# A kurtosis kernel whose first load is cut into pieces of 1024 and 3072 columns

## The chip, the cores and the metric

The kernel runs on one core of one Trainium2 chip. The metric is device time in microseconds (us): the median of several runs of one launch. The span of a profile runs from the first to the last instruction; it is about 1.7 us shorter than the measured time of the same run. All runs told here were fast: none was more than 1.5% above the fastest of its kernel. What is read inside a kernel's run comes from its one profile, so it carries that run's chance.

## The reference

```python
def reference(x):                        # x: 1024 x 8192, float32
    mean = np.mean(x, axis=-1, keepdims=True)
    std = np.std(x, axis=-1, keepdims=True)
    z = (x - mean) / (std + 1e-8)
    return (np.mean(z ** 4, axis=-1) - 3).astype(np.float32)
```

33.6 MB are read once, 4 KB are written.

## The kernel before

The rows go through in 16 groups of 64. Each row is laid over two partitions, so a group fills 128 partitions with 4096 columns (2.10 MB, 16 KB per partition). Five buffers hold the groups in flight. A group's table entry gives its rows' split over partitions, the pieces of its load, ScalarE's share of the fourth powers, and the engine that makes its mean.

```python
GROUPS = [
    (2, [4096], 1280, 'DVE'),
    (2, [4096], 1280, 'DVE'),
    (2, [4096], 768, 'DVE'),
    (2, [4096], 1536, 'DVE'),
    (2, [2304, 1792], 640, 'PE'),
    # ... seven more in two pieces, three of [1536, 1536, 1024], one in four pieces
]

def load(i):
    k, pieces = GROUPS[i][:2]
    w = n_cols // k
    xt = slots[SLOT_OF[i]]
    src = x[ROWS[i]:ROWS[i + 1], :].rearrange("r (k w) -> (r k) w", k=k)
    c = 0
    for w in pieces:
        nc.sync.dma_start(out=xt[:, c:c + w], in_=src[:, c:c + w])
        c += w

def added_halves(i, c):                  # VectorE: the mean's sum, for 'DVE' groups
    t = xts[i][:, c:]
    h = t.shape[1] // 2
    ...  # one instruction: sum of t[:, :h] + t[:, h:]

for i in range(L):                       # L = 15, the last group is treated apart
    mean(i)                              # VectorE or TensorE sums, TensorE over partitions, ScalarE copies
    square(i)                            # ScalarE, (x - mean)^2 in place
    if i >= 1:
        fourth_dve(i - 1, GROUPS[i - 1][2])   # VectorE
        load_next(i - 1)                 # the buffer of group i-1 is free: load into it
    ...
    fourth_act(i, 0, GROUPS[i][2])       # ScalarE
```

## Time and profile before

| | before |
|---|---|
| time, median of the first 3 runs | 97.04 us (97.0 to 97.14) |
| span of the profile | 95.2 us |
| ScalarE (ACT) busy | 79.8 us (84%) |
| VectorE (DVE) busy | 72.7 us (76%) |
| TensorE matmuls (PE) busy | 59.5 us (62%) |
| transfers, 16 DMA engines | 85.6% of the span, 33.56 MB |

No engine is full over the whole span, because the first 12 us are a start-up: until the first group is there nothing can be computed. After that ScalarE and the transfers are both nearly full. The waits of ScalarE say the same (engine, line, waited for: us in total, times, longest):

```profile
ACT nmu L176 <- PE mps L165: 9.4, 1, 9.4
ACT nmu L176 <- PE mps L174: 1.1, 1, 1.1
```

The reader is to see one wait for the first mean, one of 1.1 us in the middle, and no other that counts. nmu is the negative mean of a group, the last thing that ScalarE needs before it squares the group. In the lines below, junk is the unused output of VectorE's mean, tps holds TensorE's transposes, red VectorE's sums of them, and mps TensorE's sums over partitions; SPq is the issue of a load.

### The profile page before, as it was taken

Reading aid. Unit: us, or ns where it says so; the run is one execution under the profiler, and the core shown is the slowest. Engines: PE = TensorE matmul, PEld = TensorE weight load, DVE = VectorE, ACT = ScalarE, POOL = GpSimd, SP = SyncE. Lnnn points to the kernel's source line nnn. Section 1 sums busy time; section 2 is a strip of 40 time slices with the busy share of each in tenths; the row PEclk is TensorE's granted clock in tenths of the full one; section 3 lists DMA queues with packets and bytes.
Section 4 is the critical chain, followed back from the end, with each engine's and each line's share of the span. In section 5 each row is a group of like instructions: output and inputs, shape, how many; then the busy total and the mean of one; then the engine's idle time right before and its main releaser. Section 6 shows DMA issues by size and latency. Waiting matters only on the chain.

```text
span 95.2 us, 1248 instructions
## 1 busy us (share of the span) xinstructions
PE 59.5 (62%) x450; PEld 52.5 (55%) x450; DVE 72.7 (76%) x63; ACT 79.8 (84%) x88; POOL 2.7 (3%) x12
## 2 busy tenths in 40 slices
PE   0000202001089797979796969797979797989770
PEld 0000202001089696969695959686969696874330
DVE  2003529999995294979797979897999698999970
ACT  6000099999999779999999999999999999999970
POOL 6400000000000000000000000000000000000000
PEclk9999999999999999999999999999999999999999
DMA  4799999999999999999999999999999999700000
GB/s 89 268 433 433 433 427 433 440 433 394 425 429 413 425 428 429 412 422 412 433 409 430 424 419 420 415 408 403 423 412 420 416 407 408 276 15 0 0 0 1
DMA packets 4789, 33.63 MB, mean 353 GB/s; under 512 B 560, under 2 KB 560, under 8 KB 3248
## 3 DMA queue, kind: packets, MB, share of 16 engines
q1 hardware_dynamic: 4784, 33.56, 85.6%
q8 instruction: 3, 0.05, 0.2%
q14 instruction: 2, 0.02, 0.1%
HBM read 33.55 MB, written 0.00 MB: 352 GB/s over the span
## 4 chain that ended last, share of the span: by engine, by line
PE 26%; DMA 24%; ACT 18%; DVE 18%; issue 11%; SPq 0%; DVEq 0%
DMA xt<-in_x_dram 24%; PE tps L138 21%; ACT xt L182 16%; DVE xt L194 7%; DVE junk L155 7%; DVE red L144 2%; PE mps L174 2%; ACT xt L189 1%; PE pk L240 1%; PE mps L165 1%; PE pf L232 1%; SPq L132 0%; ACT nmu L176 0%; DVE q L194 0%; PE p L222 0%
## 5 line engine op out<-in xcount | busy, mean ns | idle before, releaser
L182 ACT ACTIVATE xt<-xt,nmu 128x4096 f32<-128x4096 f32 (+1 forms) x17 | 59.8, 3516 | 0.5
L194 DVE CUSTOM_DVE_ANT_0 xt<-xt 128x3456 f32<-128x3456 f32 (+8 forms) x17 | 57.5, 3386 | 2.3 <-ACT xt L182 1.9
L138 PE MATMUL tps<-ident,xt 128*128 128x128 f32 x380 | 46.9, 282 | 0.5 <-DMA xt<-in_x_dram 0.5
L138 PEld LDWEIGHTS tps<-ident,xt 128*128 128x128 f32 x380 | 43.9, 147 | 1.8 <-DMA xt<-in_x_dram 0.9
L165 PE MATMUL mps<-part,blk 128*128 128x1 f32 x8 | 2.3, 351 | 24.8 <-DVE part L155 24.8
L155 DVE CUSTOM_DVE_ANT_0 junk<-xt 128x2048 bf16<-128x2048 f32 (+1 forms) x5 | 9.6, 1915 | 9.9 <-DMA xt<-in_x_dram 9.9
L165 PEld LDWEIGHTS mps<-part,blk 128*128 128x128 f32 x8 | 2.0, 311 | 25.0 <-issue 11.0
L189 ACT ACTIVATE xt<-xt 128x640 f32<-128x640 f32 (+7 forms) x16 | 13.9, 870 | 0.5
L176 ACT COPY nmu<-mps 128x1 f32<-128x1 f32 x16 | 2.4, 148 | 10.7 <-PE mps L165 9.4
L144 DVE TENSOR_REDUCE red<-tps 128x128 f32<-128x256 f32 x12 | 5.1, 424 | 6.7 <-PE tps L138 6.6
L174 PEld LDWEIGHTS mps<-negcol,red 128*128 128x128 f32 x22 | 3.3, 188 | 8.9 <-issue 3.3
L174 PE MATMUL mps<-negcol,red 128*128 128x1 f32 x22 | 3.9, 249 | 6.5 <-DVE red L144 5.3
L203 PE MATMUL idle<-zeros 128*128 128x512 f32 x10 | 4.8, 609 | 0.0
L182 ACT ACTIVATION_READ_ACCUMULATOR xt<-xt,nmu 128x1 f32 x17 | 3.1, 184 | 0.0
L189 ACT ACTIVATION_READ_ACCUMULATOR xt<-xt 128x1 f32 x16 | 3.0, 186 | 0.0
L203 PEld LDWEIGHTS idle<-zeros 128*128 128x128 f32 x10 | 1.7, 191 | 1.4 <-issue 1.4
L67 ACT ACT_TABLE_LOAD x1 | 1.3, 1283 | 0.8 <-PEq L301 0.8
L194 DVE DVE_READ_ACCUMULATOR2_ANT q<- 128x1 f32 x17 | 1.4, 83 | 0.0
L218 PEld LDWEIGHTS p<-s,blk 128*128 128x128 f32 x4 | 0.7, 189 | 1.2 <-ACT xt L182 0.7
L66 DVE MEMSET zeros<- 128x512 f32 x1 | 0.5, 485 | 1.0 <-PEq L301 1.0
L218 PE MATMUL p<-s,blk 128*128 128x1 f32 x4 | 0.7, 234 | 0.7 <-ACT xt L182 0.7
L240 PE MATMUL pk<-blk,q 128*5 128x64 f32 (+1 forms) x10 | 1.0, 219 | 0.0
(32 smaller groups left out, 10.5 us busy)
## 6 DMA issues: line engine op xcount, KB each, us to landing
xt<-in_x_dram SPq DMA_DIRECT2D x8, 1152.0 KB, 11.4
xt<-in_x_dram SPq DMA_DIRECT2D x4, 2048.0 KB, 14.5
xt<-in_x_dram SPq DMA_DIRECT2D x8, 896.0 KB, 13.3
xt<-in_x_dram SPq DMA_DIRECT2D x7, 768.0 KB, 11.1
xt<-in_x_dram SPq DMA_DIRECT2D x3, 512.0 KB, 12.5
xt<-in_x_dram SPq DMA_DIRECT2D x1, 640.0 KB, 12.0
xt<-in_x_dram SPq DMA_DIRECT2D x1, 384.0 KB, 12.4
xt<-in_x_dram SPq DMA_DIRECT2D x1, 256.0 KB, 11.3
```

The costliest lines, as they stand in the source:

```text
L138: nc.tensor.matmul(tps, lhsT=xts[i][:, c:c + P], rhs=ident, start=c == 0, stop=c == w - P, is_transpose=True)
L144: nc.vector.tensor_reduce(out=red.rearrange("p (r k) -> p r k", k=2), in_=tps.rearrange("p (r k) -> p r k", k=2).unsqueeze(2).to_broadcast ...
L155: nc.vector.tensor_tensor_reduce(out=junk[:, :h], in0=t[:, :h], in1=t[:, h:], scale=1.0, scalar=0.0, op0=AO.add, op1=AO.add, accum_out=part)
L165: nc.tensor.matmul(mps, lhsT=blk[k], rhs=added_halves(i, 0), start=True, stop=True)
L174: nc.tensor.matmul(mps, lhsT=pair_sums(tps), rhs=negcol, start=True, stop=True)
L176: nc.scalar.copy(nmu, mps)
L182: nc.scalar.activation(out=t, in_=t, func=AF.Square, bias=nmus[i], accum_out=s2[:, j + second:j + second + 1])
L189: nc.scalar.activation(out=t, in_=t, func=AF.Square, accum_out=quads[0][:, j:j + 1])
L194: nc.vector.tensor_tensor_reduce(out=t, in0=t, in1=t, scale=1.0, scalar=0.0, op0=AO.mult, op1=AO.add, accum_out=quads[1 + second][:, j:j + 1])
L203: nc.tensor.matmul(idle, lhsT=zeros[:, :P], rhs=zeros, start=True, stop=True)
L218: nc.tensor.matmul(p2[:, n - 1:], lhsT=blk[k], rhs=s2[:, n - 1 + j:n + j], start=j == 0, stop=j == 1)
L240: nc.tensor.matmul(pk, lhsT=t, rhs=m, start=j == 0, stop=j == len(terms) - 1)
```

## The change

```diff
 GROUPS = [
-    (2, [4096], 1280, 'DVE'),
+    (2, [1024, 3072], 1280, 'DVE'),
     (2, [4096], 1280, 'DVE'),
```

The same bytes go to the same places, as two DMAs. Its likely intent is to have something of group 0 earlier. Nothing else in the program changes.

## The prediction

> **What bounds the kernel now.** I read the page's forty slices first, then the chain of waits, then ScalarE (ACT) instruction by instruction, then the start in windows.
>
> The slices, of the page:
>
> ```profile
> DVE  2003529999995294979797979897999698999970
> ACT  6000099999999779999999999999999999999970
> DMA  4799999999999999999999999999999999700000
> GB/s 89 268 433 433 433 427 433 440 433 394 425 429 413 425 428 429 412 422 412 433 409 430 424 419 420 415 408 403 423 412 420 416 407 408 276 15 0 0 0 1
> ```
>
> A slice is 95.2/40 = 2.38 us. The transfers run without a hole from slice 2 to slice 33, and ScalarE without one from slice 5, apart from a dip in slices 12 to 14. So the kernel is a start-up of about 12 us and then one long stretch in which transfers and ScalarE are both full. A change to the first load can act on the end only by moving the beginning of that stretch.
>
> The chain that ended last, its beginning (start us, length us, what):
>
> ```profile
> 0.80 0.41 SPq L132
> 1.26 12.23 DMA xt<-in_x_dram
> 13.63 2.29 DVE junk L155
> 15.93 2.50 DVE xt L194
> ...
> 26.53 0.56 PE mps L165 x2
> 27.09 5.74 PE tps L138 x32
> ```
>
> The load on it is the second issue (1.26 us), that of group 1, landing at 1.26 + 12.23 = 13.49. From there VectorE (DVE) is in series: three means (junk) with two fourth powers between them, until the mean of group 3 frees TensorE at 26.53; then TensorE's first 32 transposes, 5.74 us; then ScalarE gets the mean of group 4.
>
> The instructions in order of time, start and length first, gap before in brackets:
>
> ```profile
> 8.63 2.29 DVE L155 CUSTOM_DVE_ANT_0 junk<-xt 128x2048 bf16<-128x2048 f32 x1 [7.17 <-DMA xt<-in_x_dram]
> 11.67 0.16 ACT L176 COPY nmu<-mps 128x1 f32<-128x1 f32 x1 [9.38 <-PE mps L165]
> 15.48 0.19 ACT L182 ACTIVATION_READ_ACCUMULATOR xt<-xt,nmu 128x1 f32 x1
> 15.85 3.08 DVE L194 CUSTOM_DVE_ANT_0 xt<-xt 128x2816 f32<-128x2816 f32 x1
> 33.81 0.16 ACT L176 COPY nmu<-mps 128x1 f32<-128x1 f32 x1 [1.09 <-PE mps L174]
> ```
>
> Group 0 lands just before 8.63 and starts ScalarE at 11.67. ScalarE then has one wait of more than a microsecond, 1.09 us at 33.81, for the PE chain above; from there to 92 us it has none above 0.3 us. So group 0's landing has slack against ScalarE's later wait (1.09 us), but little on VectorE: its fourth power of group 0 starts at 15.85 and needs ScalarE's square, done at 15.48 + 0.19 = 15.67. That leaves 0.18 us.
>
> **What the Trainium skill says.** "DMA: Bandwidth & Descriptors", section "Rules for kernel authors", asks for 128 partitions and at least 1 MiB per DMA. The old first load is 2 MiB; the new pieces are 0.5 and 1.5 MiB, so one falls under it. [...]Here later loads queue behind one another, and the trace agrees only faintly: the stretches with smaller pieces move slightly fewer bytes per microsecond (below). The same page, section "Queues, rings and completion order", says that descriptors on one engine's ring are consumed in ring order. So the two pieces should follow each other as the one load did, not compete; no run here shows it yet. "Perfetto Trace Analysis", section "DMA Instruction — HWDGE (DVE, Sync)", says that the profiled length of a DMA issue ends when its descriptors are made, not when data has moved. The trace agrees: an issue is 0.41 us, its landing over 7 us after it.
>
> **The change part by part.** What is computed does not change. The order of instructions on TensorE, VectorE, ScalarE and GpSimd is the same; SyncE has one more DMA issue, and VectorE's first reduction now waits for two completions instead of one. It adds columns 0:2048 to columns 2048:4096, so the early 1024 columns release nothing.
>
> 1. *Issue time.* One issue more, 1.26 − 0.80 = 0.46 us from start to start. The first piece is issued at 0.80 as before, its second at 1.26, and group 1's load at about 1.72 instead of 1.26. The ring works on group 0 until about 8 us, so that lies wholly beside other work: 0 us. The later issues wait for buffers, not for SyncE.
>
> 2. *Transfer efficiency.* Windows (start:end, length, the engines' busy time, then granted clock, DMA share, GB/s):
>
> ```profile
> 1.80:3.40 1.60, 0.00 (x0) 0.00 (x0) 0.00 (x0) 0.48 (x2) 1.44 (x3) 1.00 1.09 225
> 3.40:8.20 4.80, 0.00 (x0) 0.00 (x0) 0.00 (x0) 0.00 (x0) 0.20 (x2) 1.00 0.96 410
> 13.00:23.00 10.00, 1.14 (x4) 1.00 (x4) 9.37 (x7) 9.87 (x11) 0.00 (x0) 1.00 1.00 426
> 23.00:43.00 20.00, 14.65 (x107) 14.05 (x108) 15.11 (x14) 18.69 (x18) 0.00 (x0) 1.00 1.01 422
> 63.00:80.00 17.00, 15.27 (x136) 14.21 (x135) 15.49 (x14) 16.75 (x18) 0.00 (x0) 1.00 1.02 415
> ```
>
> From 13 to 23 us the loads are whole groups of 2.10 MB, from 23 to 43 mostly groups in two pieces, from 63 to 80 groups in three. A group takes 2.10/0.426 = 4.92, 2.10/0.422 = 4.97 and 2.10/0.415 = 5.05 us: 0.05 to 0.08 us for each extra piece. One is added: about +0.06 us, on group 0's landing and on all that queue behind it. I take it as on the path: the second landing starts the chain.
>
> 3. *Start-up of the transfers.* Against 0.426 MB/us, the windows 1.80:3.40 and 3.40:8.20 fall short by (426 − 225) × 1.6 + (426 − 410) × 4.8 = 322 + 77 = 399 KB, which is 0.94 us. This is the engines' slow start, now met by rows of 4 KB instead of 16 KB. Nothing in the profile says whether the loss goes by time, by packet or by byte. I take it as a latency that is paid once: 0 ± 0.35 us. The ± is my choice, about a third of the loss.
>
> 4. *One wait more on VectorE.* The first piece is done before the second, so its wait is met: at most a few hundredths. I put 0.03 us, a guess; it falls on group 0 alone, inside the 0.18 us of slack, so 0 on the path.
>
> Sum: 0 + 0.06 + 0 (± 0.35) + 0 = +0.06 us. What shifts group 1's landing shifts the whole chain to ScalarE's continuous stretch and from there the end, one to one. 97.04 + 0.06 = 97.10 us.
>
> **The rivals.**
>
> *The first piece lets work begin early.* This is the likely intent. Waiting for 0.52 MB instead of 2.10 MB would take 1.57/0.43 = 3.7 us off ScalarE's wait of 9.38 us. Against it: the reduction reads both halves in one instruction. And even if group 0 were ready 1 us earlier, ScalarE would wait that much longer at 33.81, because that wait is set from group 1's landing; I give a gain of over 2% (1.94 us) almost no chance. Time if it were so: about 95 to 96.
>
> *Small rows shorten the start-up.* If the slow stretch is the time to fill each engine's first 16 KB packet, 4 KB packets get through it sooner, and half of the 0.94 us could go: about 96.6. For it: the shortfall is nearly all before 3.4 us, and all engines' shares are already busy there (1.09), so they sit in long packets. Against: the same bytes have to come through the same cold path.
>
> *Small rows lengthen it.* If in that stretch each packet pays its own delay, the eight small packets per engine (128 rows over 16 engines) pay more, perhaps half of the loss again: 97.5. Against: it needs the delay not to overlap between packets, and in the steady state the cost of extra pieces is only 0.06 us.
>
> *It is hidden anyway.* If only group 0's landing moves, by less than 0.18 us, VectorE's slack takes it all and the time stays at 97.04.
>
> **Range and chances.** The centre is 97.10. The start-up term rules the spread: −0.35 gives 96.75, +0.35 gives 97.45; the runs of before lie 0.14 us apart (97.0 to 97.14), which I add on the upper side for a chip that differs. I take 96.7 to 97.6. For a verdict beyond 2% the time would have to move by 1.94 us, twice the whole start-up loss, so within 2% gets 0.97, faster 0.015 and slower 0.015.
>
> **What would show each step right or wrong.** Group 1's load is issued near 1.72 us, and the first reduction still starts near 8.6 to 8.8, not near 4: the early piece releases nothing. ScalarE's first mean is near 11.7, and its one wait at about 33.9 is again 1.0 to 1.2 us; if it is shorter while the end stands still, only group 0 was late. The second reduction starts at 13.63 + 0.06 give or take the start-up term, and the end moves by the same amount; if it moves and the end does not, my one-to-one step is wrong. The window 1.80:3.40 shows 225 GB/s if the start-up is paid once, clearly more or less under the two rivals. The prediction is wrong if a reduction starts well before 8 us, or if a hole opens in the transfers after 10 us.

## The result, and the profile after

The changed kernel took 97.72 us (median of 6 runs, 97.3 to 97.81), the kernel before 97.08 us beside it (97.0 to 97.14). The ratio is 1.0057, 95% interval 1.0038 to 1.0076. A ratio is the mean time of one kernel's fast runs over that of the other's of the same rounds, so it is not quite the ratio of the medians. The kernel became about 0.6 us slower: within 2%, as forecast, but outside the stated range of 96.7 to 97.6.

The slices of the changed kernel:

```profile
DMA  2999999999999999999999999999999999500000
GB/s 41 290 420 464 403 430 430 430 437 411 425 434 419 416 422 429 406 424 423 429 411 422 431 420 421 405 409 420 413 416 417 409 407 408 203 14 0 0 0 1
```

The stretch without holes is still there. The first slice shows 41 GB/s instead of 89, but this view books all bytes of a packet in the slice in which it starts, so packets of 4 KB and of 16 KB cannot be compared there.

The chain that ended last, in part:

```profile
1.26 7.81 DMA xt<-in_x_dram
9.22 2.29 DVE junk L155
...
12.45 3.81 ACT xt L182 x2
...
41.58 10.88 DMA xt<-in_x_dram
52.46 0.14 issue
52.59 3.86 PE tps L138 x32
```

It now begins with group 0's second piece (issued at 1.26, landing at 9.07) and runs through ScalarE, where before it began with group 1's load and ran through VectorE. Later it passes through a load and TensorE's transposes. The chain before did too (a load issued at 51.28 us landed at 61.97, then TensorE's transposes at 62.11), in the part that the prediction left out; that part proves to matter.

The windows of the start (columns as in the prediction, the last is GB/s):

```profile
1.80:3.40 1.60, 0.00 (x0) 0.00 (x0) 0.00 (x0) 0.48 (x2) 1.45 (x3) 1.00 0.92 189
3.40:8.20 4.80, 0.00 (x0) 0.00 (x0) 0.00 (x0) 0.00 (x0) 0.21 (x2) 1.00 1.00 405
```

189 and 405 against 225 and 410: (225 − 189) × 1.6 + (410 − 405) × 4.8 = 82 KB fewer, 0.19 us at 0.426 MB/us. The windows too book a packet where it starts, which makes the 225 too high (a DMA share of 1.09 is a sign of it). With the bytes spread over each packet's own time, the same traces give 164 GB/s before and 171 after in the first window, and 410 and 391 in the second: 77 KB fewer by 8.2 us, 0.18 us. The sum stands, but the loss lies after 3.4 us. There the 4 KB packets of the first piece took 213 to 220 ns in the mean (3.5 to 4.5 us), where undisturbed ones take 159 (e7 below); the 16 KB packets of the kernel before took 619 ns between 4 and 5 us and 611 later.

Instructions in order of time:

```profile
9.22 2.29 DVE L155 CUSTOM_DVE_ANT_0 junk<-xt 128x2048 bf16<-128x2048 f32 x1 [7.76 <-DMA xt<-in_x_dram]
12.26 0.16 ACT L176 COPY nmu<-mps 128x1 f32<-128x1 f32 x1 [9.97 <-PE mps L165]
33.64 0.16 ACT L176 COPY nmu<-mps 128x1 f32<-128x1 f32 x1 [0.39 <-PE mps L174]
67.57 0.16 ACT L176 COPY nmu<-mps 128x1 f32<-128x1 f32 x1 [0.40 <-PE mps L174]
```

The first reduction starts 0.59 us later than before (8.63), and ScalarE's first mean as much later (11.67). Of the 0.59, 0.46 are the landing (8.61 before, 9.07 now); the other 0.13 lie between landing and start, 0.02 us before and 0.15 now. But by 33.64 us ScalarE is 0.17 us *ahead* of the kernel before (33.81). The lateness comes back later, as a wait at 67.57 us that the kernel before did not have.

**Why the fill is late by more than the bytes say.** In the traces each load ends with 16 packets of 4 bytes, one completion for each DMA engine, and the landing follows the last of them (8.25 us, landing at 8.61). The counts of packets in two windows show when these came. Kernel before, windows 7.6 to 8.3 and 8.3 to 8.8 us:

```profile
DMA packets 35, 0.31 MB, mean 445 GB/s; under 512 B 16, under 2 KB 16, under 8 KB 16
DMA packets 12, 0.20 MB, mean 393 GB/s; under 512 B 0, under 2 KB 0, under 8 KB 0
```

Changed kernel, the same windows:

```profile
DMA packets 32, 0.30 MB, mean 433 GB/s; under 512 B 11, under 2 KB 11, under 8 KB 11
DMA packets 19, 0.23 MB, mean 459 GB/s; under 512 B 5, under 2 KB 5, under 8 KB 5
```

"under 512 B" counts the completions. Before, all 16 engines are done by 8.3 us; in the changed kernel 5 of them are not. In the trace the completions of group 0 reach from 7.62 to 8.25 us before and from 7.70 to 8.74 us after: the first engine is 0.08 us later, the last 0.48. Groups 1 to 3 keep both spreads, 0.63 and 1.03 us, because from group to group the first and the last completion come 4.86 us apart alike: no engine catches up.

**Where it reaches the end.** TensorE's transposes of group 4, 10 and 11, in order of time. Before:

```profile
26.95 5.87 PE L138 MATMUL tps<-ident,xt 128*128 128x128 f32 x32
...
57.13 3.85 PE L138 MATMUL tps<-ident,xt 128*128 128x128 f32 x32 [0.17 <-DMA xt<-in_x_dram]
...
62.11 3.82 PE L138 MATMUL tps<-ident,xt 128*128 128x128 f32 x32 [0.17 <-DMA xt<-in_x_dram]
```

After:

```profile
27.43 5.21 PE L138 MATMUL tps<-ident,xt 128*128 128x128 f32 x32
...
57.57 3.85 PE L138 MATMUL tps<-ident,xt 128*128 128x128 f32 x32 [0.17 <-DMA xt<-in_x_dram]
...
62.55 4.02 PE L138 MATMUL tps<-ident,xt 128*128 128x128 f32 x32 [0.17 <-DMA xt<-in_x_dram]
```

Group 4 starts 0.48 us later but takes 5.21 us instead of 5.87, so that delay vanishes. These are TensorE's first long work after a wait; later sets take 3.7 to 4.0 us. The Trainium skill, "TensorE: Matmul & The Clock Gate", section "Part 1: The HAM clock gate (the "warmup" mystery)", says that TensorE is slow until it has been busy for a while, and that the point where it speeds up varies with a free-running window. The 5.1 to 6.6 us seen for this same set over the profiles agree with that; the granted clock in the page shows full speed there, so the cause is not shown here.

At groups 10 and 11 TensorE waits for the first piece of the load, in both kernels, and there it is 0.44 us late again. Group 11 also has the longer set (4.02), because its second piece landed at 64.78 us instead of 64.14, 0.64 us later. From there the two kernels run in step: ScalarE's mean of group 15 starts at 85.97 and 86.61, again 0.64 us apart.

### The profile page after: what moved, and what is told of

It reads as the page before. It is cut to its first block, busy times and chain, and to the rows that moved or that the text cites. A ratio compares the mean times of both kernels' runs of the same rounds, so it can differ in the third digit from the quotient of the medians.

```text
span 96.0 us, 1253 instructions
## 1 busy us (share of the span) xinstructions
PE 59.4 (62%) x450; PEld 51.8 (54%) x450; DVE 72.6 (76%) x63; ACT 79.9 (83%) x88; POOL 2.7 (3%) x12
## 4 chain that ended last, share of the span: by engine, by line
ACT 39%; PE 20%; DMA 19%; DVE 11%; issue 7%; SPq 0%; DVEq 0%; ACTq 0%
ACT xt L182 32%; DMA xt<-in_x_dram 19%; PE tps L138 15%; DVE xt L194 6%; ACT xt L189 6%; DVE junk L155 2%; PE mps L174 2%; DVE red L144 2%; ACT nmu L176 1%; PE pk L240 1%; PE mps L165 1%; PE pf L232 1%; SPq L132 0%; PE p L222 0%; DVE kr L242 0%
## 5 line engine op out<-in xcount | busy, mean ns | idle before, releaser
L138 PEld LDWEIGHTS tps<-ident,xt 128*128 128x128 f32 x380 | 43.2, 145 | 2.6 <-DMA xt<-in_x_dram 1.5
```

The source lines that it names most:

```text
L138: nc.tensor.matmul(tps, lhsT=xts[i][:, c:c + P], rhs=ident, start=c == 0, stop=c == w - P, is_transpose=True)
```

## The experiments

Three theories were open. *Uneven start:* something about small rows lets the DMA engines come out of the start further apart. *Extra issue or transfer:* one more issue, or its descriptors made beside the start, costs about half a microsecond. *Second wait:* the first reduction, which now waits for two completions, pays for it. After the first four runs a fourth took shape: *addresses*, that engines which all read the same quarter of each 16 KB at once slow one another. The packet records hold no addresses, so this is tested by moving the reads, not seen.

One table for all profiles; "landing" is issue plus time to landing in the trace, "mean 15" the start of ScalarE's last mean. The time is the median, the ratio is to the kernel before on the same chip in the same rounds.

| kernel | group 0 lands | group 3 lands | group 11 lands | mean 15 | time | ratio |
|---|---|---|---|---|---|---|
| before | 8.61 | 23.29 | 64.14 | 85.97 | 97.08 | |
| changed | 9.07 | 23.75 | 64.78 | 86.61 | 97.72 | 1.0057 |
| e1 group 1 split | 8.67 | 24.20 | 64.56 | 87.03 | 97.65 | 1.0067 |
| e2 3072 + 1024 | 8.87 | 23.57 | 64.93 | 86.75 | 97.68 | 1.0056 |
| e3 2048 + 2048 | 8.42 | 23.11 | 64.12 | 85.94 | 97.20 | 1.0008 |
| e4 4 × 1024 | 9.22 | 23.91 | 65.13 | 86.95 | 97.98 | 1.0092 |
| e5 before again | 8.42 | 23.07 | 64.37 | 86.19 | 97.14 | 0.9997 |
| e6 changed again | 9.32 | 24.00 | 64.64 | 86.93 | 97.72 | 1.0057 |
| e7 as e1, dense | 8.43 | 23.18 | 64.15 | 86.06 | 97.31 | 1.0017 |
| e8 as changed, dense | 8.00 | 22.69 | 64.58 | 86.40 | 97.18 | 1.0005 |
| e9 before, held | 8.56 | 23.21 | 64.08 | 85.90 | 97.03 | 0.9995 |
| e10 changed, held | 9.03 | 23.71 | 64.95 | 86.77 | 97.96 | 1.0085 |

### e1: split group 1 instead of group 0

```diff
-    (2, [1024, 3072], 1280, 'DVE'),
-    (2, [4096], 1280, 'DVE'),
+    (2, [4096], 1280, 'DVE'),
+    (2, [1024, 3072], 1280, 'DVE'),
```

> Group 1 is split into 1024 and 3072 columns instead of group 0. Uneven start (small rows during the slow start of the transfers make the DMA engines come out of it further apart, and a landing waits for the slowest): the first rows are whole again, so group 0 lands as before, first reduction at 8.63 +- 0.1, time 97.1 to 97.2. Extra transfer (one more issue and completion costs about 0.5 us wherever it stands in the first groups): first reduction at 8.63, second about 0.4 later than 13.63, time 97.6 to 97.8.

Measured: 97.65 us, ratio 1.0067 (1.0047 to 1.0088). Group 0 landed as before (8.67), but from group 0's landing to group 3's it took 24.20 − 8.67 = 15.53 us instead of 14.68. This was a miss for the uneven start: the cost follows the split to a group that is loaded after the start (its completions come from 9.14 us on). The extra transfer seemed to win in the time, though the second reduction was 0.94 us later (14.57), not 0.4. But in the trace the 4 KB packets themselves are slow there: 159 ns until 8 us, then 198 ns in the mean between 8 and 9 us and 275 between 9 and 10, up to 380.

### e2: the large piece first

```diff
-    (2, [1024, 3072], 1280, 'DVE'),
+    (2, [3072, 1024], 1280, 'DVE'),
```

> Group 0 in 3072 and 1024 columns: still two pieces, two completions and one more issue, but the rows in the slow start are 12 KB. Uneven start: first reduction at 8.7 to 8.9, time 97.1 to 97.3. Extra transfer, or the second wait of the first reduction: 9.2 and 97.6 to 97.8, as in the changed kernel.

Measured: 97.68 us, ratio 1.0056 (1.0041 to 1.0071), first reduction at 9.01. The reduction lies between the forecasts (8.7 to 8.9, and 9.2), the landing moved less than in the changed kernel (8.87), and the time did not follow: a miss for the uneven start. The spread of the completions is that of the kernel before (7.94 to 8.55 us, 0.61): here all engines are late, by about 0.3 us. The 12 KB packets that started between 4.5 and 7 us took 538 ns in the mean instead of 460.

### e3: two equal halves

```diff
-    (2, [1024, 3072], 1280, 'DVE'),
+    (2, [2048, 2048], 1280, 'DVE'),
```

> Group 0 in two pieces of 2048 columns, rows of 8 KB. Uneven start: between whole rows and 4 KB rows, first reduction at 8.8 to 9.1, time 97.2 to 97.5. Extra transfer or second wait: 9.2 and 97.6 to 97.8.

Measured: 97.20 us, ratio 1.0008 (0.9992 to 1.0024): no difference is seen. This run has the same extra issue, the same extra transfer and the same second wait as the changed kernel. So none of the three, by itself, is the cost, and the second-wait theory falls for good. What differs is the size of the pieces, and with it which columns are read together. The reduction at 8.56 was also earlier than the uneven start had said (8.8 to 9.1).

### e4: four pieces of 1024 columns

```diff
-    (2, [1024, 3072], 1280, 'DVE'),
+    (2, [1024, 1024, 1024, 1024], 1280, 'DVE'),
```

> Group 0 in four pieces of 1024 columns: the start sees the same 4 KB rows as in the changed kernel, with two more transfers, issues and waits behind. Uneven start: as the changed kernel plus two times 0.06 to 0.1 us, first reduction at 9.3 to 9.4, time 97.7 to 97.9. Extra transfer (0.5 us each): first reduction near 10.2, time 98.4 to 98.9. Second wait (0.5 us once or per wait): 9.2 to 10.2.

Measured: 97.98 us, ratio 1.0092 (1.0072 to 1.0113), first reduction at 9.38. A cost of half a microsecond for each extra transfer would have given over 98.4. The time is 0.08 us above the forecast of the uneven start, the reduction inside it. Group 0's landing, 9.22, lies between the two looks at the changed kernel (9.07 and 9.32), so the profiles show no cost of the two further pieces.

### e5 and e6: both kernels again

No edit.

> The kernel before, unchanged, for a second look at its start: every theory expects 97.0 to 97.2. How far its first landing (8.61 in the first look, as issue plus time to landing) and that of the load of group 3 (23.29) move from run to run tells how much of a shift in one profile is chance: if by less than 0.15 us, the +0.46 of the changed kernel is its own.

> The changed kernel, unchanged: 97.3 to 97.8. If its start costs the same in each run, group 3 lands again at 23.6 to 23.9; if the cost is chance in the order in which the engines come out of the start, anywhere from 23.3 to 24.0.

Measured: 97.14 us (ratio 0.9997, 0.9979 to 1.0014) and 97.72 us (1.0057, 1.0033 to 1.0081). The landing of group 3 moves by chance more than I had set as the limit: 23.29 and 23.07 for the kernel before, 23.75 and 24.00 for the changed one. With the held kernels below, three looks each give 23.07 to 23.29 and 23.71 to 24.00. They do not overlap, so the cost is the change's own; its size in one profile is uncertain by some 0.2 us. The same windows 7.6 to 8.3 and 8.3 to 9.1 us in the second look at the changed kernel show 10 completions and then 6:

```profile
DMA packets 32, 0.32 MB, mean 462 GB/s; under 512 B 10, under 2 KB 10, under 8 KB 10
...
DMA packets 30, 0.39 MB, mean 486 GB/s; under 512 B 6, under 2 KB 6, under 8 KB 6
```

In this profile the end came by the other way. TensorE's first set took 6.56 us, and ScalarE's wait was long:

```profile
35.24 0.16 ACT L176 COPY nmu<-mps 128x1 f32<-128x1 f32 x1 [1.74 <-PE mps L174]
```

From there the profile shows no wait of ScalarE as far as its mean of group 11 at 68.16 us, and its last mean came 86.93 − 64.64 = 22.29 us after group 11's landing. In nine of the twelve profiles that distance is 21.82 or 21.83 us; the three others are e1 (22.47), e6 (22.29) and e7 (21.91), the ones in which the last mean came 51.7 us after that of group 4, the shortest distance seen (52.16 before, 52.97 changed). So two paths end close together: ScalarE from group 4 on, and the transfers to group 11. In each run the later one decides.

### e7 and e8: the same pieces from dense stretches of memory

For one group, piece after piece of consecutive memory is read: 512 KB, then 1.5 MB, instead of 4 KB and 12 KB out of each 16 KB. Packet sizes and counts, issues and places in SBUF stay. Rows are mixed up, so the result is wrong.

```diff
+        flat = x[ROWS[i]:ROWS[i + 1], :].rearrange("r c -> (r c)")
         for w in pieces:
-            nc.sync.dma_start(out=xt[:, c:c + w], in_=src[:, c:c + w])
+            part = src[:, c:c + w]
+            if i == 1:                   # e8: i == 0
+                part = flat[c * P:(c + w) * P].rearrange("(p w) -> p w", w=w)
+            nc.sync.dma_start(out=xt[:, c:c + w], in_=part)
```

> As the kernel with group 1 split, but the two pieces of group 1 read dense stretches of memory (512 KB, then 1.5 MB) instead of 4 KB and 12 KB out of every 16 KB; packet sizes, counts, issues and places in SBUF stay, the result is wrong on purpose. Address theory (engines that all read the same quarter of each 16 KB slow one another): the 4 KB packets of group 1 all take 159 to 165 ns, where the first look had means of 198 and 275 ns between 8 and 10 us; group 3 lands 0.4 to 0.7 us earlier than 24.20 and the time is 97.1 to 97.3. Packet-size theory (small packets in a row are slow by themselves, or the extra transfer costs it): packets up to 380 ns again, 97.5 to 97.8.

> As the changed kernel, but its two pieces of group 0 read dense stretches of memory; the result is wrong on purpose. Address theory: fewer slow packets in the start, group 3 lands at 23.2 to 23.5 instead of 23.75, time 97.0 to 97.3. Packet-size or extra-issue theory: as the changed kernel, 97.5 to 97.8.

Measured, e7: 97.31 us, ratio 1.0017 (1.0000 to 1.0033) where e1 had 1.0067. The window 8.2 to 10.6 us, in which group 1's small piece goes through, in e1:

```profile
DMA packets 148, 0.92 MB, mean 384 GB/s; under 512 B 17, under 2 KB 17, under 8 KB 101
```

and in e7:

```profile
DMA packets 158, 1.09 MB, mean 454 GB/s; under 512 B 16, under 2 KB 16, under 8 KB 96
```

"under 8 KB" less "under 512 B" is the number of 4 KB packets, 84 and 80: nearly the same work, at 384 and 454 GB/s. In e7 each of those packets took 159 ns. From group 0's landing to group 3's it took 23.18 − 8.43 = 14.75 us, 0.07 us more than before, where e1 took 15.53. Group 3 landed 1.02 us earlier than in e1, more than the forecast 0.4 to 0.7, and the time is 0.01 us above the forecast.

Measured, e8: 97.18 us, ratio 1.0005 (0.9980 to 1.0030) where the changed kernel had 1.0057. Its start:

```profile
1.80:3.40 1.60, 0.00 (x0) 0.00 (x0) 0.00 (x0) 0.48 (x2) 1.44 (x3) 1.00 1.03 330
```

330 GB/s, against 189 in the changed kernel with the same 4 KB packets (by each packet's own time 291 and 171, and 164 in the kernel before). Group 0 landed at 8.00 us, 1.07 us earlier than in the changed kernel and 0.61 earlier than before. So small packets are not slow by themselves, and the start is not a fixed latency: both follow which addresses are read. That the engines slow one another by reading alike at the same moment is the likely reason, but not shown: the dense reads also spare each engine the jumps from row to row. Against the jumps alone speaks e3, which jumps too and costs nothing clear. Group 3 landed at 22.69, earlier than I had expected for either theory.

But the time did not fall below the kernel before. In e8 the packets of 9 KB of group 4's first piece took 388 to 417 ns in the mean between 22 and 24 us, where the kernel before has 347, and the load of group 4 ended no earlier (its first piece landed at 26.20 us, before at 26.07). Of this run the profile was also the slowest of six (96.86 to 97.50).

### e9 and e10: nothing else issued during the start

A memset into group 1's buffer, on GpSimd after its constants, holds the issues of groups 1 to 4 back to about 3.6 us. e9 is the kernel before with it, e10 the changed one.

```diff
+    nc.gpsimd.memset(slots[1][:, 0:1], 0.0)
     load_next(-1)
```

> The kernel before, with the issues of groups 1 to 4 held back to about 3.6 us by one small memset on GpSimd into group 1's buffer, so that nothing else is issued while group 0 starts. Issue theory (descriptors of later loads slow the start): window 1.80:3.40 above the 225 GB/s of the kernel before, group 3 lands before 23.0. Address theory: window and landings as before (225 GB/s, 23.0 to 23.3), time 97.0 to 97.2.

> The changed kernel with the same hold: only the two issues of group 0 go out before about 3.6 us. Issue theory: the loss goes, group 3 lands near 23.3, time 97.0 to 97.2. Address theory: the loss stays, window 1.80:3.40 near 188 GB/s, group 3 at 23.6 to 24.0, time 97.5 to 97.8.

Measured: 97.03 us (ratio 0.9995, 0.9974 to 1.0015) and 97.96 us (1.0085, 1.0062 to 1.0108). In e9 the first window shows 236 GB/s, one packet of 16 KB more than the 225 before, and group 3 landed at 23.21, not before 23.0. Without any other issue beside it the start of the split load is as slow as with them:

```profile
1.80:3.40 1.60, 0.00 (x0) 0.00 (x0) 0.00 (x0) 0.48 (x2) 1.44 (x3) 1.00 0.77 189
```

The issue theory falls. The time of e10 was above what I had expected of the address theory (97.5 to 97.8); its landings are those of the changed kernel up to group 3, and the rest of the surplus is not explained.

No version beat the kernel before by a clear margin. e8 points to a faster start, but reads wrong rows, and its gain was gone by group 4.

## Why the prediction was right or wrong

**No work begins early, right.** The first reduction started at 9.22 us, not near 4. The two pieces followed each other: the completions of the first came from 4.03 to 5.08 us, those of the second from 7.70 to 8.74.

**Issue time, right.** Group 1's load is issued later beside running transfers, at no cost; e9 and e10 move issues by far more without a gain.

**Transfer efficiency, +0.06 us, right in size where it can be seen.** In e7 the first completion of the split group 1's load comes 4.91 us after the first of group 0's, the last 4.91 us after the last, and those of the whole groups behind it 4.86 us apart: 0.05 us for one piece more. Between profiles a shift of this size is lost in chance.

**Start-up of the transfers, 0 ± 0.35 us, the step that failed.** I took it "as a latency that is paid once". The runs showed in its place a cost that depends on which addresses are read, and that does not belong to the start-up: the same split of group 1 costs as much (e1, 97.65 us), and dense reads take it away (e7, 97.31; e8, 97.18). Group 0 landed 0.46 us later in the first look and three looks each of split and whole give group 3 on average at 23.82 and 23.19, 0.63 us apart. Less the 0.06 us of efficiency, the term measured about +0.57 us, outside my ±0.35. Part of the error was to count bytes: the windows lose only 0.19 us of bytes, but a landing waits for the slowest engine, and in the changed kernel the spread of the engines grew from 0.63 to 1.03 us (in the second looks 0.41 and 1.35). The loss of 0.94 us from which the range was taken was itself read from windows that book packets where they start; for the same reason the sign "225 GB/s if the start-up is paid once" could not decide.

**Second wait on VectorE, a guess of 0.03 us, too small but off the path as said.** From landing to start it was 0.02 us in both looks at the kernel before and 0.14 to 0.16 in e2, e3, e4, e8 and the changed kernel, so about 0.13 us, inside the 0.18 us of slack that the prediction found. e3 has it and its time shows no loss.

**"Shifts the whole chain one to one", wrong as told.** The chain through VectorE and group 4 was late by 0.48 us and lost that again, when TensorE's first set ran faster; ScalarE's wait near 33.9 was 0.39 us, not 1.0 to 1.2, and yet the end moved. The delay reached the end by another way, which I had not named: every later load is as late, and at groups 10 and 11 TensorE waits for loads. In the first look 0.43 us at the landing of group 10's first piece (57.00 to 57.43) became 0.64 us at that of group 11's last. That extra 0.21 us falls where the trace shows two packets of the profile's "instruction" kind, on queues of their own, at about 61 us; which engine gets them would decide whether the slowest is held up. This was not tested and stays open.

**The rivals.** "Small rows lengthen it", at 97.5, came nearest in the time. Its mechanism, a delay per packet, is wrong: e7 and e8 have the same packets without the loss. "Small rows shorten the start-up" did not come true for columns, but e8 shows that dense small rows can: group 0 landed 0.61 us earlier than before, though the time did not fall. "Hidden anyway" failed because group 1's landing moved too (second reduction at 14.10 instead of 13.63).

One small slip of reading in the prediction: ScalarE's dip is in slices 13 and 14 (counted from 0), not 12 to 14; nothing rests on it.

What stays open is which address bits count. Pieces of 1024 or 3072 columns out of 4096 cost, halves of 2048 did not (e3). The later pieces of 1024 columns in groups 12 to 14 do not show it: their 4 KB packets take 163 ns in the mean between 66 and 80 us (half of them at most 160). By then the engines are further out of step: in the kernel before a packet of the "instruction" kind held one engine for 1.1 us at 41.8 us, and the completions of the load that landed next lie 1.81 us apart instead of 0.64. That fits the address theory, but it was not tested by itself.

## What to carry to other kernels

Here a load landed when its slowest DMA engine was done, so judge a split by when the last completion comes, not by bytes per microsecond alone: in the changed kernel the engines came apart, in e2 all were late together. Before you compare windows, ask where the view books a packet that crosses their edge. Cutting a load by columns changes which addresses are read; a dense read of the same sizes tells, in one run, whether that or the packet size is the cost. Before you call a shift one to one, look for the next place where the late resource is waited for: a delay can be swallowed on one path and come back on another.

## What the Trainium skill lacked or had wrong

- "DMA: Bandwidth & Descriptors", section "Rules for kernel authors": it asks for at least 1 MiB per DMA. A 0.5 MiB piece of a dense stretch cost nothing clear here (e7, ratio 1.0017), the same piece of columns did (e1, 1.0067); the rule by size does not tell the two apart.
- The same page, section "Latency and other measured facts", has a row on large row pitches (512 KiB and more, between HBM tensors). It has nothing on rows 16 KB apart that are read in part: 384 GB/s in e1 against 454 in e7 over the same 2.4 us.
- The same page, section "Why a DMA increments its semaphore by 16 and not by 1", has the count of completions by engine, but not that a lag once gained stays: 1.03 us between first and last engine in group 0 and still in group 3.
- Packets of the profile's "instruction" kind run on the same engines as the loads: one of 16 KB took 1.10 us at 41.8 us, and the spread of the next completions went from 0.64 to 1.81 us. It belongs to "Runtime: NRT & Kernel Launch", section "Instruction fetch mechanics", which does not give what this does to a stream of loads.
- No page that I read has the slow start of a core's transfers depend on addresses: 189 and 330 GB/s between 1.8 and 3.4 us for the same 4 KB packets, from columns (the changed kernel) and from a dense stretch (e8).
